# Adaln parameters of a transformer kernel: whole float32 matmuls in place of split parts

## The chip, the cores and the metric

The kernel runs on one core of a Trainium2 chip. Its time is the device time of one launch in microseconds (us). It has four compute engines with queues of their own, each of which works through its instructions in the order in which they stand: TensorE (PE, with its weight loads shown apart as PEld), VectorE (DVE), ScalarE (ACT) and GpSimd (POOL). SyncE (SP) issues most of the DMAs, also in order.

## The reference, cut to what matters

The reference is a transformer of two blocks on 256 tokens of 1024 features. The first block begins with the adaln parameters: a vector of conditions goes through silu and a matrix of 1024 x 6144, and the results shift, scale and gate the features.

```python
def adaln_params(cond, w_mod, b_mod):
    mod = jax.nn.silu(cond) @ w_mod + b_mod
    return mod.reshape(cond.shape[0], N_MOD, 1, cond.shape[-1])
...
mod = adaln_params(c, w_mod[layer], b_mod[layer])
mod_c = adaln_params(c_ctx[None, :], w_mod[layer], b_mod[layer])
h = modulate(x, norm1_g[layer], mod[:, 0], mod[:, 1])
hc = modulate(ctx, norm1_g[layer], mod_c[:, 0], mod_c[:, 1])
```

So the first 2048 parameters (shift and scale of the first norm) are wanted for two columns, c and c_ctx, and nothing of the first block's projections can start before shift and scale are there. Everything is float32.

## The kernel before

Activations lie transposed (features on the partitions, tokens on the free axis). Weights come from DRAM in tiles of 128 x 1024 (512 KB). A float32 product is carried by float32r passes: `split_w` (lines 107 to 116) makes of each raw weight tile a part hi by a cast on ACT (line 111) and a rest lo by a subtraction on DVE or POOL (line 115), and matmuls with hi and lo are summed in PSUM. A matmul of two operands that are plain float32 is one line in the program and two instructions in the trace.

The stretch around the change is the first 100 us. Three kinds of work share it:

- The adaln tiles. `mod_group` (line 299) runs for g = 0 to 3, four tiles `mraw` each; the text calls these sixteen tiles T0 to T15. Of each, hi and lo are made (on ACT and on DVE), and the two condition columns, as hi and lo parts in `sc4` of four columns, are the stationary operand while 512 weight columns move (line 308): 64 matmuls in all. The four rows of a group's result are copied out of PSUM (line 318, `mods`) and turned onto the partitions by small float32 matmuls with `fold` (line 323), and line 324 adds the bias into `mod`. The turn of groups 0 to 2 is issued in the next group.
- The filler. At places named in `PLACES`, one more tile of `mem_ahead` is issued, work that hangs on nothing near: keys of the memory attention, eight weight tiles with 24 matmuls each at line 137 (F0 to F7 here; F0's rest lo is made on DVE, of the others on POOL), then values, four tiles with 24 matmuls each at line 172 before the gates (V0 to V3). Two F tiles share the one PSUM bank `fill`, which line 1040 (`kvt`) empties on DVE.
- The norms of x and ctxT (squares on ACT at lines 214 and 217, sums on DVE at line 219, matmuls with ones at line 228) and the decay matrices of the retention (lines 388 to 416: a chain of small DVE steps `dlacc`, then, head by head, two DVE steps `decayt`, exponentials on ACT, and an addition on POOL).

When the last group is in `mod`, `scale_of` makes `modA`, `modulated` makes the normed input h in eight chunks (lines 246 to 248), and the gate blocks (line 137, `mm<-hh,whi`) begin the dense part of the kernel.

Within each engine the order is that of a scheduler which works over the whole program before it runs: it puts instructions of independent parts into one fixed row for each engine. At run time an instruction waits for its operands, and everything behind it on its engine waits with it. A tile's buffers also set the order: `raw` has three, the parts `whi` three and `wlo` two, `mraw` four.

Of the kernel before, what the change touches and what calls it, by code (L numbers as in the profile page):

```python
"""A two-part transformer in one launch.

Activations lie transposed, features on the partitions and tokens on the free axis, and stay in
SBUF from the first norm to the last. Weights stream through SBUF once. A float32 product is
carried by three float32r passes: each operand is split into a part that float32r holds exactly
and the rest (hi + lo), and hi*hi + hi*lo + lo*hi are accumulated in PSUM.
"""
# [8 lines left out]
F32 = mybir.dt.float32  # L16
F32R = mybir.dt.float32r
# [11 lines left out]
KC = 8  # L29
# [10 lines left out]
MRAW = 4  # L40
# [29 lines left out]
class Build:  # L70
# [15 lines left out]
    def banks(self, ctx, name):  # L86
        """The banks of one phase: mm and, by the phase, sc and aux or pairs of banks."""
        self.ps = ctx.enter_context(self.tc.tile_pool(name="psum" + name, bufs=2, space=PSUM))
# [5 lines left out]
    def after(self, ins, other):  # L94
        """Issue order only: no wait."""
        self.tc.add_manual_dep(ins.ins, other.ins.name,
                               mybir.DependencyInfo(mybir.DependencyClass.NoSync, mybir.DependencyReason.DATA),
                               reason="order")

# [18 lines left out]
    def weight(self, src, lo=None):  # L118
        """hi and lo of a weight tile. lo: the engine of the subtraction."""
# [7 lines left out]
    def mm3(self, out, pairs, first=True, last=True, late=False):  # L127
        """out += sum of w^T x over (w_hi, w_lo, x_hi, x_lo), three passes each; late: pair by pair."""
# [10 lines left out]
    def fill(self, n):  # L139
        """n tiles of the work that depends on nothing near."""  # L140
        for _ in range(n):
            next(self.filler, None)
# [6 lines left out]
    def block(self, out, src, x, cols=slice(None), lo=None, late=False, w=None):  # L149
        """out[128 n, tokens] = W block^T x, the weights stationary."""  # L150
# [8 lines left out]
    def natural_steps(self, tag, srcs, toks, done, lo=None):  # L159
        """x^T W with the tokens stationary, 256 columns of W (two tiles of srcs) at a time; two  # L160
        token blocks share a bank. done(n, i, bank) takes the columns n of the token blocks 2i, 2i + 1."""
# [26 lines left out]
    def rstd(self, pool, sums, n, tag, shape=(P, T), bufs=1, a=None, y=None, tables=False, behind=None):  # L188
        """(sums / n + eps) ** -0.5, a Newton step after the tables."""
# [19 lines left out]
    def track(self, x, m, tags=("acc", "accsq"), bufs=2):  # L209
        """Adds the squares of chunk m of eight to the sum over chunks; the last stays apart."""  # L210
# [10 lines left out]
    def tracked_norm(self, pool, tag, bank="aux", urgent=False, last=None, **kw):  # L221
        """rstd over the features of the chunks tracked, the same on every partition; last: behind the matmuls
        so far."""
# [17 lines left out]
    def modulated(self, pool, tags, x, r, A, Bv, h, cols):  # L241
        """h[:, :, cols] = x * r * A + B, split."""
# [8 lines left out]
    def gained(self, pool, x, gi, name="h"):  # L251
        """x * g (no rstd yet), split."""
# [37 lines left out]
    def mod_start(self, pool):  # L290
# [4 lines left out]
        self.sc4 = pool.tile([P, KC, 4], F32R, name="sc4")  # L295
        nc.vector.tensor_copy(self.sc4[:, :, 0:2], self.sc)
        nc.vector.tensor_sub(self.sc4[:, :, 2:4], self.sc, self.sc4[:, :, 0:2])

    def mod_group(self, pool, g):
        """512 of the adaln parameters, for c and for c_ctx: the rows of o are hi c, hi c_ctx, lo c, lo c_ctx."""  # L300
        nc, io = self.nc, self.io
        o = self.psum([P, 512])
        for q in range(4):
            wh, wl = self.split_w(self.raw(io["w_mod1"][g, q], pool, "mraw", MRAW), pool, "m", "v")
            for i, w in enumerate((wh, wl)):
                for kk in range(2):
                    k, m = 2 * q + kk, 4 - 2 * i
                    nc.tensor.matmul(o[:m], self.sc4[:, k, :m], w[:, kk * 512:kk * 512 + 512],
                                     start=k == 0 and i == 0, stop=k == 7, skip_group_check=True)
            if g == 0 and q == 0:  # L310
                self.load_constants()
                self.fold = pool.tile([4, 2], F32, name="fold")
                nc.vector.tensor_add(self.fold, self.ident[0:4, 0:2], self.ident[0:4, 2:4])
# [3 lines left out]
        s = pool.tile([4, 512], F32, name="mods", tag="mods", bufs=2)  # L317
        nc.vector.tensor_copy(s, o[:4])

        def turn():  # L320
            tr = self.psum([P, 4, 2])
            for j in range(4):
                nc.tensor.matmul(tr[:, j, :], s[:, j * P:(j + 1) * P], self.fold, start=True, stop=True)
            nc.vector.tensor_tensor(self.mod[:, 4 * g:4 * g + 4, :], tr,
                                    self.bmod[:, 4 * g:4 * g + 4, None].to_broadcast([P, 4, 2]), op=OP.add)

        if g == 3:
            turn()
        else:
            self.folding.append(turn)  # L330

    def mod_rest(self, pool, groups):
        """gate1, shift2, scale2, gate2 for c, a piece at a time."""
# [36 lines left out]
    def rope_out(self, pool, q, out, cos, sin):  # L370
        """out = q * cos + rot(q) * sin for q [128, 256] in SBUF; sin has the signs of rot, which swaps the halves
        of every 32 partitions."""
# [7 lines left out]
    def decay(self, pool, M):  # L380
        """M [j, t] for j in x and in ctx, by head: [128, 4 heads, 4 key chunks, 256]. The logarithms of the
        rates are not positive, so the smaller of the two exponents is the one for the sign of the distance."""
# [36 lines left out]
    def lam(self, pool, ls):  # L419
        """-lambda in the last column of ls."""  # L420
# [10 lines left out]
    def mixer(self):  # L431
        nc, io, tc = self.nc, self.io, self.tc
        with ExitStack() as ctx:
# [64 lines left out]
            def values(base):  # L498
                """[128 keys, 4 key blocks, 512], 256 columns at a time."""
# [10 lines left out]
            # differential attention  # L510
# [71 lines left out]
            # retention  # L582
# [54 lines left out]
    def residual(self, name, act, gate=None, nk=KC):  # L637
        """x += gate * (W^T act)."""
# [12 lines left out]
    def head_squared(self, pool, y):  # L651
        """y out of its bank, and its squares."""
# [7 lines left out]
    def head_norm(self, pool, y, g, out=None):  # L660
        """rms_norm over the partitions of y, times g; y as head_squared gives it."""
# [10 lines left out]
    def squared(self, pool, o, n):  # L672
        """o out of its bank, and its squares."""
# [8 lines left out]
    def qk_norm(self, pool, z, bd, g, out, n):  # L682
        """rms_norm over each 64 partitions of z as squared gives it: the first 256 columns in place, the others
        to out."""
# [11 lines left out]
    def peer(self):  # L696
        nc, io = self.nc, self.io
        with ExitStack() as ctx:
# [123 lines left out]
            def turn():  # L822
                """The selected keys by slot, and each gate as a float32r part and the ratio of its rest to that."""
# [30 lines left out]
            def hot(g):  # L854
                """The one-hot rows of the slots of TG tokens, with the gates in one of them, for two tokens at a time."""
# [92 lines left out]
            def collect(th):  # L948
                """x += gate * the transposed rows of acc, for the tokens of th."""
# [33 lines left out]
    def mem_kv(self, pool, mpool, l, key, value, norm=None):  # L983
        """k^T [128 d, 8, 256 m] and v [128 m, 2, 1024], two heads or 256 columns at a time; key and value
# [633 lines left out]
```

## Time and profile before

| what | value |
|---|---|
| median of 3 runs | 1934.56 us (1934.15 to 1935.23) |
| profiled execution, its span | 1934.6 us |
| PE busy over the span | 1838.1 us (95%) |
| DVE busy over the span | 1465.7 us (76%) |
| ACT busy over the span | 1043.2 us (54%) |
| POOL busy over the span | 587.3 us (30%) |
| first gate matmul | 95.51 us after the span's start |

Busy time is an engine's own; what sets the end is the chain of work, in which each step waits for one before it. In a row of the timeline the first two numbers are the start and the length in us, then come engine, line, operation, the tile written and those read, shapes, and how many such instructions in a row were merged (x8). A row that merges many shows the length from the first one's start to the last one's end. In a row of windows each engine has its busy us and, in brackets, how many instructions began; PEclk is the granted clock of TensorE, 1.00 for 2.4 GHz and 0.50 for 1.2 GHz.

### The profile page before, as it was taken

How to read it: one execution, taken by the hardware profiler on the slowest of the kernel's cores; microseconds unless marked ns; L12 is line 12 of the kernel's file. 1: busy time of each engine (PE TensorE's matmuls, PEld its weight loads, DVE VectorE, ACT ScalarE, POOL GpSimd, SP SyncE). 2: the span in 40 equal slices, each digit the busy share in tenths (PEclk: the TensorE clock that was granted, in tenths of full speed). 3: DMA queues.
4: the chain of work that ended last, by engine and by line, in shares of the span. 5: the costliest groups of instructions: out<-in, count | busy, mean ns of one | idle time of the engine just before them, and what ended most of it. 6: DMA issues, size and time to landing. Idle time of an engine off the chain costs nothing.

```text
span 1934.6 us, 34858 instructions
## 1 busy us (share of the span) xinstructions
PE 1838.1 (95%) x13232; PEld 1717.9 (89%) x13232; DVE 1465.7 (76%) x2646; ACT 1043.2 (54%) x1775; POOL 587.3 (30%) x508
## 2 busy tenths in 40 slices
PE   5899999994999999999999998999999999999997
PEld 4697788994999999878888878999999998999997
DVE  8988966999988999865555568676765578677664
ACT  5645534542777777554554455455554544555543
POOL 2511113782888999400000004222000213110001
PEclk8999999997999999999999998999999999999999
DMA  7672434452444444655555555553555553435553
GB/s 261 218 250 93 137 131 154 170 179 76 167 161 164 164 153 160 225 195 194 196 195 191 192 184 177 185 185 132 195 187 187 187 179 130 158 127 186 187 191 124
DMA packets 99768, 335.15 MB, mean 173 GB/s; under 512 B 12400, under 2 KB 13456, under 8 KB 99216
## 3 DMA queue, kind: packets, MB, share of 16 engines
q1 hardware_dynamic: 98160, 330.68, 49.5%
q8 instruction: 105, 1.72, 0.4%
q10 hardware_dynamic: 1440, 2.23, 0.3%
q14 instruction: 63, 0.52, 0.1%
HBM read 329.59 MB, written 3.28 MB: 172 GB/s over the span
## 4 chain that ended last, share of the span: by engine, by line
PE 69%; DVE 16%; POOL 9%; DMA 2%; issue 2%; ACT 2%; SPq 0%; DVEq 0%; ACTq 0%; POOLq 0%
PE mm L137 40%; PE pair L945 17%; POOL ohA L861 5%; PE mm L172 4%; POOL slots L882 3%; PE fill L137 2%; DVE wlo L115 2%; PE fill L172 2%; DVE slots L798 1%; DVE slots L795 1%; PE pair L876 1%; PE sc L137 1%; DVE slots L773 1%; PE aux L137 1%; DVE mlo L115 1%
## 5 line engine op out<-in xcount | busy, mean ns | idle before, releaser
L111 ACT CAST whi<-raw 128x1024 fp32r<-128x1024 f32 x564 | 591.4, 1050 | 517.5 <-PE mm L137 261.0
L115 DVE TENSOR_TENSOR wlo<-raw,whi 128x1024 fp32r<-128x1024 f32 x490 | 623.9, 1276 | 297.7 <-PE pair L945 129.3
L115 POOL TENSOR_TENSOR wlo<-raw,whi 128x1024 fp32r<-128x1024 f32 x74 | 186.5, 2522 | 199.1 <-PE mm L137 109.0
L861 POOL TENSOR_SCALAR ohA<-iota,selT 128x128 fp32r<-128x128 f32 x256 | 191.1, 762 | 53.2 <-ACT selT L829 32.5
L219 POOL TENSOR_TENSOR acc<-acc,accsq 128x256 f32<-128x256 f32 x42 | 37.9, 903 | 497.9 <-ACT accsq L217 497.9
L137 PE MATMUL mm<-hh,whi 128*128 128x256 f32 (+1 forms) x1184 | 180.0, 289 | 6.2 <-DVE ct L1243 4.4
L137 PE MATMUL mm<-hl,whi 128*128 128x256 f32 (+1 forms) x1184 | 177.1, 287 | 1.0 <-DVE hl L262 0.9
L137 PE MATMUL mm<-hh,wlo 128*128 128x256 f32 (+1 forms) x1184 | 175.7, 286 | 0.6 <-DVE wlo L115 0.6
L137 PE MATMUL mm<-h2h,whi 128*128 128x256 f32 x1152 | 167.6, 288 | 4.1 <-ACT h2h L247 4.0
L137 PEld LDWEIGHTS mm<-hh,whi 128*128 128x128 f32 x1184 | 156.5, 190 | 11.1 <-issue 6.8
L137 PE MATMUL mm<-h2h,wlo 128*128 128x256 f32 x1152 | 163.4, 284 | 0.0
L137 PE MATMUL mm<-h2l,whi 128*128 128x256 f32 x1152 | 162.4, 284 | 0.0
L945 PE MATMUL pair<-whi,acth 128*128 128x512 f32 x512 | 158.4, 391 | 1.0 <-ACT acth L937 1.0
L137 PEld LDWEIGHTS mm<-hh,wlo 128*128 128x128 f32 x1184 | 155.0, 190 | 4.4 <-issue 1.5
L945 PE MATMUL pair<-whi,actl 128*128 128x512 f32 x512 | 158.2, 390 | 0.3 <-DVE actl L938 0.3
L137 PEld LDWEIGHTS mm<-hl,whi 128*128 128x128 f32 x1184 | 155.2, 190 | 3.4 <-DVE hl L262 1.6
L945 PE MATMUL pair<-wlo,acth 128*128 128x512 f32 x512 | 157.8, 389 | 0.0
L137 PEld LDWEIGHTS mm<-h2h,whi 128*128 128x128 f32 x1152 | 151.9, 195 | 5.0 <-ACT h2h L247 4.8
L137 PEld LDWEIGHTS mm<-h2h,wlo 128*128 128x128 f32 x1152 | 150.1, 193 | 0.0
L137 PEld LDWEIGHTS mm<-h2l,whi 128*128 128x128 f32 x1152 | 149.3, 193 | 0.0
L1083 POOL TENSOR_TENSOR memk0l<-kvt,memk0h 128x512 fp32r<-128x512 f32 x4 | 6.4, 1611 | 378.9 <-ACT memk0h L1082 378.9
L945 PEld LDWEIGHTS pair<-whi,acth 128*128 128x128 f32 x512 | 95.5, 188 | 22.1 <-ACT acth L937 2.6
(416 smaller groups left out, 3454.2 us busy)
## 6 DMA issues: line engine op xcount, KB each, us to landing
raw<-peer_u SPq DMA_DIRECT2D x128, 512.0 KB, 3.5
raw<-peer_v SPq DMA_DIRECT2D x128, 512.0 KB, 3.4
raw<-ffn_gu SPq DMA_DIRECT2D x88, 512.0 KB, 3.6
raw<-ffn_dn SPq DMA_DIRECT2D x44, 512.0 KB, 3.5
raw<-w_mod SPq DMA_DIRECT2D x64, 256.0 KB, 4.1
raw<-conv_wi SPq DMA_DIRECT2D x24, 512.0 KB, 3.5
raw<-mem_wk SPq DMA_DIRECT2D x16, 512.0 KB, 4.5
mraw<-w_mod SPq DMA_DIRECT2D x16, 512.0 KB, 6.4
```

The costliest lines, as they stand in the source:

```text
L111: self.hi_copy = nc.scalar.copy(hi, raw)
L115: (nc.vector if plan == "v" else nc.gpsimd).tensor_sub(lo, raw, hi)
L137: self.matmul = nc.tensor.matmul(out, a, b, start=first and j == 0, stop=last and j == 3 * n - 1)
L172: self.matmul = nc.tensor.matmul(outs[i // 2][:, i % 2], a[:, k, :], b[:, w], start=k == 0 and s == 0 and i % 2 == 0, stop=k == 7 and s == ...
L219: self.adder.tensor_add(self.acc, self.acc, self.last)
L773: nc.vector.tensor_tensor(cand, vv[:, :, 0, :, None].to_broadcast([P, 2, 16, 16]), vv[:, :, 1, None, :].to_broadcast([P, 2, 16, 16]), op=O ...
L795: nc.vector.tensor_tensor(one, pb[:, :, :, None].to_broadcast([P, 2, 16, 16]), self.iota[:, None, None, 0:16].to_broadcast([P, 2, 16, 16]) ...
L798: nc.vector.tensor_tensor(one, one, ii[:, :, side, None, :].to_broadcast([P, 2, 16, 16]), op=OP.mult)
L861: nc.gpsimd.tensor_scalar(A[:, i], self.iota, selT[:, 1, t:t + 1], None, op0=OP.is_equal)
L876: nc.tensor.matmul(o[:, 2 * j + i], A[:, i], Bt[:, i], start=True, stop=True)
L882: getattr(nc, GMUL).tensor_mul(sl, lo[:, :, :done], sl)
L945: nc.tensor.matmul(acc[th][:, dh], x[:, tsl], wt[:, dh * 512:dh * 512 + 512], start=c == 0 and s == 0, stop=c == NCH - 1 and s == 2)
```

## The change

The tiles `mraw` are not split any more. The weights are the stationary operand (128 x 128 of a tile), and the two condition columns `sc` move, both plain float32; the result stands on the partitions at once, so the copy `mods`, the operand `fold` and the turn go, and line 315 adds the bias straight from the sum's bank. `MRAW` is 8 in place of 4. Docstrings and comments go too, which moves line numbers up by nine in the rest of the file.

```diff
-MRAW = 4
+MRAW = 8
...
-        self.sc4 = pool.tile([P, KC, 4], F32R, name="sc4")
-        nc.vector.tensor_copy(self.sc4[:, :, 0:2], self.sc)
-        nc.vector.tensor_sub(self.sc4[:, :, 2:4], self.sc, self.sc4[:, :, 0:2])
...
-        o = self.psum([P, 512])
+        o = self.psum([P, 4, 2])
         for q in range(4):
-            wh, wl = self.split_w(self.raw(io["w_mod1"][g, q], pool, "mraw", MRAW), pool, "m", "v")
-            for i, w in enumerate((wh, wl)):
-                for kk in range(2):
-                    k, m = 2 * q + kk, 4 - 2 * i
-                    nc.tensor.matmul(o[:m], self.sc4[:, k, :m], w[:, kk * 512:kk * 512 + 512],
-                                     start=k == 0 and i == 0, stop=k == 7, skip_group_check=True)
+            w = self.raw(io["w_mod1"][g, q], pool, "mraw", MRAW)
+            for kk in range(2):
+                k = 2 * q + kk
+                for j in range(4):
+                    c = kk * 512 + j * P
+                    nc.tensor.matmul(o[:, j, :], w[:, c:c + P], self.sc[:, k, :], start=k == 0 and j == 0,
+                                     stop=k == 7, skip_group_check=True)
             if g == 0 and q == 0:
                 self.load_constants()
-                self.fold = pool.tile([4, 2], F32, name="fold")
-                nc.vector.tensor_add(self.fold, self.ident[0:4, 0:2], self.ident[0:4, 2:4])
...
-        s = pool.tile([4, 512], F32, name="mods", tag="mods", bufs=2)
-        nc.vector.tensor_copy(s, o[:4])
-
-        def turn():
-            tr = self.psum([P, 4, 2])
-            for j in range(4):
-                nc.tensor.matmul(tr[:, j, :], s[:, j * P:(j + 1) * P], self.fold, start=True, stop=True)
-            nc.vector.tensor_tensor(self.mod[:, 4 * g:4 * g + 4, :], tr,
+
+        def place():
+            nc.vector.tensor_tensor(self.mod[:, 4 * g:4 * g + 4, :], o,
                                     self.bmod[:, 4 * g:4 * g + 4, None].to_broadcast([P, 4, 2]), op=OP.add)
 
         if g == 3:
-            turn()
+            place()
         else:
-            self.folding.append(turn)
+            self.folding.append(place)
```

The scheduler makes new rows of this. On DVE, around the first group's result and the first emptying of the filler's bank (`kvt`), there stood before:

```order
L394 TENSOR_TENSOR dlz_277<-dlz 128x8
L397 TENSOR_TENSOR dlacc<-dlacc,dlz_277 128x8
L398 TENSOR_SCALAR dlacc<-dlacc 128x8
L115 TENSOR_TENSOR mlo<-mraw,mhi 128x1024
L204 SCALAR_TENSOR_TENSOR mracc<-mracc,mry 128x256
...
L206 SCALAR_TENSOR_TENSOR mry<-mracc,mry 128x256
L397 TENSOR_TENSOR dlacc<-dlacc,dlz_277 128x8
L318 COPY mods<-mm 4x512
L1040 TENSOR_TENSOR kvt<-fill,mry 128x512
```

And now, at the same place:

```order
L385 TENSOR_TENSOR dlz_272<-dlz 128x8
L206 SCALAR_TENSOR_TENSOR mry<-mracc,mry 128x256
L388 TENSOR_TENSOR dlacc<-dlacc,dlz_272 128x8
L315 TENSOR_TENSOR mod<-mm,b_mod 128x8
L1031 TENSOR_TENSOR kvt<-fill,mry 128x512
L389 TENSOR_SCALAR dlacc<-dlacc 128x8
```

The addition into `mod`, which needs all of T0 to T3, stands where the copy `mods` stood, ahead of `kvt` and of nearly the whole chain `dlacc`; five of its steps stood ahead of `kvt` before and one does now.

On ACT, the cast `whi` of F3 and what stands ahead of it (the squares `acc` and `accsq`, the exponentials `decayM` and `decaye`) were before:

```order
L111 CAST mhi<-mraw 128x1024
L217 ACTIVATE accsq<-ctxT 128x256
L413 ACTIVATE decayM<-dist,dlfar,dllg 128x512
L111 CAST mhi<-mraw 128x1024
L415 ACTIVATE decaye<-dist,dlfar,dlneg 128x512
L111 CAST whi<-raw 128x1024
```

And now:

```order
L406 ACTIVATE decaye<-dist,dlfar,dlneg 128x512
L403 ACTIVATE decayM<-decayt 128x512
L214 ACTIVATE acc<-x 128x256
L217 ACTIVATE accsq<-x 128x256 x2
L214 ACTIVATE acc<-ctxT 128x256
L404 ACTIVATE decayM<-dist,dlfar,dllg 128x512
L217 ACTIVATE accsq<-x 128x256 x2
L111 CAST whi<-raw 128x1024
```

One head's `decaye` stood ahead of F3's cast before; now three heads' do (this is the third), with all the squares of x up to the fifth.

On PE, the last adaln tiles among the filler's matmuls stood before, from the second tile of group 2 on:

```order
L308 MATMUL mm<-mhi,sc_108 4x512 x2
L323 MATMUL mm<-fold,mods 128x2 x4
L308 MATMUL mm<-mlo,sc_108 2x512 x2
L308 MATMUL mm<-mhi,sc_108 4x512 x2
L137 MATMUL fill<-hmh,whi 128x256
L308 MATMUL mm<-mlo,sc_108 2x512 x2
L137 MATMUL fill<-hmh,whi 128x256 x7
L137 MATMUL fill<-hmh,wlo 128x256 x8
```

And now, from the last tile of group 1 to the last of group 3:

```order
L306 MATMUL mm<-sc,mraw 128x2 x32
L228 MATMUL aux<-acc,ones 128x256
L137 MATMUL fill<-hmh,whi 128x256 x8
L306 MATMUL mm<-sc,mraw 128x2
L137 MATMUL fill<-hmh,wlo 128x256 x8
L137 MATMUL fill<-hml,whi 128x256 x8
L306 MATMUL mm<-sc,mraw 128x2 x15
L137 MATMUL fill<-hmh,whi 128x256 x8
L306 MATMUL mm<-sc,mraw 128x2
L137 MATMUL fill<-hmh,wlo 128x256 x8
L137 MATMUL fill<-hml,whi 128x256 x8
L306 MATMUL mm<-sc,mraw 128x2 x23
```

Pairs of wide matmuls spread among the filler became runs of up to 32 narrow ones (four tiles), of which each is two instructions.

## Rows read from the trace of the kernel before

**Rows 1.** Windows of 10 us, with the view's heading row.
```profile
core 0: us, PE busy (x) PEld busy (x) DVE busy (x) ACT busy (x) POOL busy (x), PEclk, DMA share, GB/s
20.00:30.00 10.00, 9.20 (x42) 6.89 (x42) 9.67 (x23) 3.44 (x8) 2.40 (x1) 0.74 0.98 398
...
100.00:110.00 10.00, 10.00 (x85) 10.00 (x85) 10.00 (x19) 8.37 (x12) 0.00 (x0) 0.99 0.82 285
```

**Rows 2.** Chain of waits, 0 to 130 us: shares; then start, length, engine, line.
```profile
by line: PE mm L137 15.9%; DVE mlo L115 9.5%; PE mm L172 7.4%; DMA mraw<-w_mod 7.0%; issue 6.9%; PE fill L137 5.3%; DVE acc L219 4.7%; DVE modt L246 4.1%; DVE hl L248 3.8%; PE mm L308 3.0%; PE mm L323 2.4%; DVE decayt L411 2.3%; DVE mracc L
...
95.51 6.54 PE mm L137 x40
```

**Rows 3.** Instructions by line: count, then duration min/median/max in ns, first and last start.
```profile
L115 DVE TENSOR_TENSOR mlo<-mraw,mhi x16: 1203/1212/3324, 15.5 to 70.9; 128x1024 fp32r<-128x1024 f32 x16
...
L111 ACT CAST mhi<-mraw x16: 1027/1034/1050, 12.6 to 67.9; 128x1024 fp32r<-128x1024 f32 x16
...
L318 DVE COPY mods<-mm x4: 669/672/679, 29.2 to 77.2; 4x512 f32<-4x512 f32 x4
...
L323 PE MATMUL mm<-fold,mods x32: 246/246/267, 36.3 to 78.7; 4*128 4x2 f32 x32
```

**Rows 4.** Timeline of PE and PEld: runs of two-column matmuls, and weight loads.
```profile
57.50 1.05 PE L323 MATMUL mm<-fold,mods 4*128 4x2 f32 x8 [1.24 <-DVE mods L318]
...
131.81 0.95 PE L341 MATMUL mm<-ones,macc 128*128 128x2 f32 x8
...
8.19 0.29 PEld L137 LDWEIGHTS fill<-hmh,wlo 128*128 128x128 f32 x1 [0.15 <-DVE wlo L115]
...
11.53 0.19 PEld L137 LDWEIGHTS fill<-hmh,wlo 128*128 128x128 f32 x1
```

**Rows 5.** Timeline of PE: filler matmuls of F1 (two rows) and F3, then T6.
```profile
22.85 1.91 PE L137 MATMUL fill<-hmh,wlo 128*128 128x256 f32 x8
...
24.55 1.38 PE L137 MATMUL fill<-hml,whi 128*128 128x256 f32 x8
...
44.40 1.09 PE L137 MATMUL fill<-hml,whi 128*128 128x256 f32 x8
45.33 0.63 PE L308 MATMUL mm<-mhi,sc 128*4 128x512 f32 x2
```

**Rows 6.** Timeline of ACT, DVE and POOL: cast of F2, kvt, decay steps.
```profile
24.44 1.04 ACT L111 CAST whi<-raw 128x1024 fp32r<-128x1024 f32 x1
...
29.76 0.67 DVE L1040 TENSOR_TENSOR kvt<-fill,mry 128x512 f32<-128x512 f32 x1
...
31.15 0.42 DVE L219 TENSOR_TENSOR acc<-acc,accsq 128x256 f32<-128x256 f32 x1
31.49 0.16 DVE L397 TENSOR_TENSOR dlacc<-dlacc,dlz 128x8 f32<-128x8 f32 x1
...
37.37 0.81 ACT L415 ACTIVATE decaye<-dist,dlfar,dlneg 128x512 f32<-128x512 f32 x1
...
46.83 0.63 ACT L412 ACTIVATE decayM<-decayt 128x512 f32<-128x512 f32 x1 [4.13 <-DVE decayt L411]
...
38.26 2.29 POOL L416 TENSOR_TENSOR decayM<-decayM,decaye 128x512 f32<-128x512 f32 x1 [10.30 <-ACT decaye L415]
...
41.02 2.57 DVE L410 TENSOR_SCALAR decayt<-dist,dlneg 128x512 f32<-128x512 f32 x1
...
46.06 0.74 DVE L411 SCALAR_TENSOR_TENSOR decayt<-dist,dllg,decayt 128x512 f32<-128x512 f32 x1
```

**Rows 7.** Windows of 2 us around a run of L323.
```profile
56.00:58.00 2.00, 0.76 (x7) 0.50 (x5) 2.00 (x4) 2.00 (x3) 2.00 (x2) 1.00 0.86 244
...
60.00:62.00 2.00, 2.00 (x9) 1.80 (x8) 2.00 (x2) 0.71 (x1) 0.82 (x1) 0.50 0.95 369
```

**Rows 8.** Timeline of DVE and POOL after the last group.
```profile
78.98 0.17 DVE L324 TENSOR_TENSOR mod<-mm,b_mod 128x8 f32<-128x8 f32 x1 [1.14 <-PE mm L323]
...
81.94 2.70 POOL L115 TENSOR_TENSOR wlo<-raw,whi 128x1024 fp32r<-128x1024 f32 x1 [5.50 <-PE fill L172]
```

## The prediction, made before the change was run

> **What bounds the kernel now.** I read the windows first, then the chain of waits, then the engines' rows around the adaln tiles. From 100 us on PE is full (10.00 of 10 us) at a granted clock of 0.99 [rows 1], and the gate blocks that start this stretch begin at 95.51 [rows 2]. What matters here is therefore one number, the start of the gates: what comes behind it hangs on it, and I carry a shift of it to the end one for one. Ahead of it PE has gaps, and DVE is close to full (9.67 of 10 us from 20 to 30) [rows 1]. The chain from 0 to 130 us gives 9.5% to the subtractions `mlo`, 3.0% and 2.4% to the matmuls of lines 308 and 323 [rows 2]: what the change removes is on the path, with DVE ahead of PE. The last group is in `mod` at 78.98 + 0.17 = 79.2 us [rows 8], and the gates follow 16.4 us later.
>
> **What goes.** Sixteen `mlo` of 1.21 us, four `mods` of 0.67 us: 22.0 us of DVE. Sixteen casts of 1.03 us: 16.5 us of ACT. On PE 64 wide matmuls and 32 instructions of the turn [rows 3, 5]. With `mlo` gone what is late next is not the data but the order of what is left, below.
>
> **What comes.** 128 matmuls of 128 x 128 weights against two columns, two instructions each, since the turn's 16 of the program are 32 in the trace [rows 3]. Price of one: the run of eight at line 341, with 128 x 128 weights, is 0.95 us long, one of them 0.25 as at line 323, so (0.95 - 0.25) / 7 = 0.100 us from one to the next; at line 323 it is 0.115 [rows 4]. The run at 57.50 began at a clock of 1.00 [rows 7]. Such a run at the low clock is not in the trace: a weight load is 0.19 us after the clock rose and 0.29 before [rows 4], and eight filler matmuls take 24.55 - 22.85 = 1.70 us from start to start at the low clock, 0.213 each, and 45.33 - 44.40 = 0.93 at the high one, 0.116 each [rows 5]. So 0.100 is the low bound, twice that, 0.20, the high one, and a tile of 16 costs 1.6 to 3.3 us; all sixteen 25.6 to 52 us. I let the clock decide between them (step 3). The 64 wide ones, two in 0.63 us [rows 5], were 20 us at most, with the turn's 32 x 0.115 = 3.7 on top: PE's work does not shrink, and at the low clock it more than doubles.
>
> The Trainium skill, "TensorE: Matmul & The Clock Gate", section "LDWEIGHTS (loading the stationary operand)", gives a load's time as its columns over 1.2, which is 107 ns for 128 at either clock. Here loads of one size took 0.19 and 0.29 us, so the trace does not agree that the clock leaves them alone. By that rule, an estimate, the narrow matmuls of step 3 would cost 17 us whatever the clock, and the sum would come out near +11 instead of +16.
>
> **Step 1: the first group.** T0 starts behind F0 at 12.7 as before. F1 starts about 0.9 us earlier, since one `mlo` ahead of the memory norm on DVE is gone; it ended at 24.55 + 1.38 = 25.9 [rows 5], now 25.0. T2 and T3 follow, 3.2 us: T3 ends at 28.2 (31.6 at the low clock). Only then can DVE add the first group into `mod`, and `kvt` stands right behind it: 0.17 + 0.67 and a little, 29.1; before it started at 29.76 [rows 6]. No gain so far. But ACT's cast for F2 now stands behind `kvt`'s DMA, so it runs near 29.2, where before it ran at 24.44 [rows 6], and POOL's rest comes 2.7 us [rows 8] behind it.
>
> **Step 2: F3 behind the decay chain.** The row of ACT puts F3's cast behind three heads of exponentials and five squares of x, and these wait for DVE. From `kvt` at 29.1: 17 steps `dlacc` at about 0.20 and three more, 4.1 us, to 33.2. Then head by head, since `decayt` and `decaye` have two buffers between them: two exponentials 1.6; an addition on POOL 2.29; an exponential 0.81; an addition 2.29; an exponential 0.81 and 0.63; the fourth head's two `decayt`, 2.57 beside POOL and 0.74; two sums of 0.42 with the squares behind them, 1.3; the cast 1.03 [rows 6]: 14.1, less 0.7 for overlaps of neighbours on ACT, 13.4. F3's cast ends at 46.6, POOL's rest at 49.2, and its last 16 matmuls take 1.9 to 3.4 us: F3 ends at 51.5. It ended at 44.40 + 1.09 = 45.5 [rows 5]. What hid all this before was that F3's cast stood behind one head only. PE meanwhile has just F2, T4 and T5, and idles for some 5 us.
>
> **Step 3: F3's end to T15's end.** PE then has, in this order: T6, the norm of x, F4, F5, T7 to T10, the norm of ctxT, F6, T11, T12, F7, T13 to T15. At the high clock: 96 filler matmuls at 0.117, 11.2 us; 160 narrow ones at 0.100, 16.0. Apart from these 1.8 us for the two norms and 3.1 for a wait: F6's cast stands behind the ctxT norm's logarithm on ACT, so PE waits for a DVE step, that logarithm, the cast (1.03) and, after eight matmuls, POOL's 2.70. Sum 32 at the high clock; at the low one 2 x 27.2 + 4.9 = 59. Which of these? Before the clock fell to 0.50 (60 to 62 us), PE was busy in 56 to 58 for only 0.76 us [rows 7], and from 57.50 on that was the run of line 323 [rows 4]; in 20 to 30 us, with the filler beside waits, it was 0.74 on average [rows 1]. The new runs are longer (up to 64 instructions) than any of these. I take 0.72, next to that row: 27.2 / 0.72 = 37.8, plus 4.9, 43 us. T15 ends at 51.5 + 43 = 94.5; before, the same stretch ended at 79.0.
>
> **Step 4: from T15 to the gates.** V0's cast now stands behind the first chunks of h on ACT, so all four V tiles come after T15: POOL's first rest starts 3.0 us after `mod` (as the one at 81.94 did, after 78.98), four at 2.70 make 10.8, and V3's 24 matmuls 2.8 [rows 8]: 16.6. The modulation on DVE runs beside it, with fewer norm steps in between. It was 16.4, so nothing is won: gates at 94.7 + 16.6 = 111.3 against 95.5.
>
> **Sum.** +15.8 us. The span is 1934.6 and the median 1934.56, so no correction: 1950.4. Eight `mraw` buffers cost nothing and bring nothing, since SP's later tiles stand behind `raw` tiles which wait for POOL's rests of F2 to F4 (steps 1 and 2); T7 to T15 are there by the time PE comes to them.
>
> **Rivals.**
> - *The clock stays high.* Back-to-back narrow matmuls may keep it. Then step 3 is 32, F3 ends at 51.1, T15 at 83.2, gates at 100.0: +4.5, 1939. For it: a run of line 323 itself began at 1.00. Against it: what the clock did after that run [rows 7]. The Trainium skill, same page, section "What's actually happening", says the gate follows how busy PE has been of late; if a stream of loads counts as busy, this is that case, and no run here shows so long a stream.
> - *The clock stays low throughout.* Step 3 is 59, T3 3.4 later and F3 at 56.0, so T15 ends at 115.0 and the gates start at 131.8: +36, 1971. Against it: F4 with F5, and F6, are dense filler, and dense filler raised it before.
> - *DVE's time is all that counts* (the faster side). If steps 1 and 2 do not bite, because ACT and POOL come to F2's and F3's tiles in time, the chain's 9.5% of 130 us goes: 12.4 us, and PE's work (25.6 against 23.7 at most) hides in its gaps: 1922. It decides if F3 ends before about 40 us. For it: DVE is near full before 80 us. Against it: rows 6, the fixed order.
> - *Part of it is made up later*: PE's backlog after the gates finds DVE further ahead, the shift shrinks to under 4 us: 1936. Against it: PE is full from 100 us on [rows 1].
>
> **Chances.** The forecast (mixed clock, +7 to +26) 0.57; high clock 0.12, which lies on the edge and which I count 0.08 slower, 0.04 the same; low clock 0.08; faster rival 0.16; made up later 0.07, of it 0.06 the same. About 0.2%, 3.9 us, is what can be told from no change. Slower 0.57 + 0.08 + 0.08 + 0.01 = 0.74, same 0.10, faster 0.16. The range 1928 to 1967 leaves out most of the faster rival and of the low clock; the forecast's own range is 1942 to 1961.
>
> **What would show it.** Right: the first `mod` row near 28 us with `kvt` right behind; F3's cast on ACT near 46; PE idle ahead of F3; runs of line 306 stepping at 0.10 in one clock and about 0.2 in the other, and the granted clock falling during T7 to T10; T15's end past 85; gates near 111. Wrong: F3 ending before 42, or T15 before 79, or the narrow matmuls stepping otherwise than 0.10 to 0.21; and a gap before the gates much shorter than 16 us.

## The result, and the profile after

The changed kernel takes 1959.87 us (median of 4 runs, 1958.97 to 1961.74) against 1934.36 for the kernel before beside it: 1.0133 times, 95% interval 1.0119 to 1.0147, or +25.5 us. The forecast was slower, 1950, with a range up to 1967: the direction and the range hold, the size was 15.8 and is 25.5. The profiled execution has a span of 1958.0 us against 1934.6. Its time was 1959.78 us: in every run on record the time is 1.7 to 2.3 us above the span of the same execution. By this, an estimate, the execution profiled before took some 1936.4 us, which is 2 us above its kernel's median, so "no correction" in the prediction's sum was wrong by that much, and +23.4 in the spans goes with +25.5 in the medians.

First the windows of 10 us of the changed kernel, columns as in [rows 1]:

```profile
40.00:50.00 10.00, 4.50 (x22) 4.21 (x23) 8.18 (x9) 6.67 (x14) 6.12 (x3) 0.54 0.44 162
...
60.00:70.00 10.00, 9.34 (x54) 8.61 (x53) 0.77 (x3) 0.17 (x1) 0.00 (x0) 0.64 0.53 183
...
80.00:90.00 10.00, 10.00 (x63) 10.00 (x62) 0.69 (x1) 0.00 (x0) 0.00 (x0) 0.66 0.11 44
...
100.00:110.00 10.00, 6.49 (x41) 6.28 (x39) 9.82 (x12) 3.94 (x7) 6.42 (x3) 0.81 0.57 194
```

DVE, which was near full before [rows 1], has 0.77 and 0.69 us of work in two of these windows (9.45 and 10.00 in the kernel before): the change did free it, and nothing used it. PE either waits (busy for 4.50 of 10 us from 40 to 50) or is full, or nearly so, at a clock of about 0.65. The timeline of PE, in which the last column is the idle time ahead and what ended it:

```profile
12.58 1.84 PE L306 MATMUL mm<-sc,mraw 128*128 128x2 f32 x16
...
15.04 3.58 PE L306 MATMUL mm<-sc,mraw 128*128 128x2 f32 x16 [0.62 <-DMA mraw<-w_mod]
...
45.07 2.07 PE L137 MATMUL fill<-hmh,whi 128*128 128x256 f32 x8 [5.76 <-ACT whi L111]
...
49.34 1.10 PE L137 MATMUL fill<-hml,whi 128*128 128x256 f32 x8
...
58.54 9.73 PE L306 MATMUL mm<-sc,mraw 128*128 128x2 f32 x64
...
71.23 2.08 PE L137 MATMUL fill<-hmh,whi 128*128 128x256 f32 x8 [1.90 <-ACT whi L111]
...
95.78 0.58 PE L172 MATMUL fill<-whi,hmh 128*128 128x256 f32 x1 [2.86 <-ACT whi L111]
...
98.37 0.58 PE L172 MATMUL fill<-wlo,hmh 128*128 128x256 f32 x1 [1.80 <-POOL wlo L115]
...
103.01 0.41 PE L172 MATMUL fill<-wlo,hmh 128*128 128x256 f32 x1
...
111.16 0.58 PE L172 MATMUL fill<-whi,hmh 128*128 128x256 f32 x1 [4.67 <-ACT kvt L1035]
...
118.23 1.12 PE L137 MATMUL mm<-hh,whi 128*128 128x256 f32 x8
...
133.14 2.00 PE L137 MATMUL mm<-hh,whi 128*128 128x512 f32 x8
```

These are T0 at the high clock (1.00) and T1 at the low one (0.51), F3's wait, F3's end (it was 44.40 + 1.09 in [rows 5], now 50.4), T7 to T10 in one run, F6, V0's two waits, V0's last matmul, V2's wait, and the gates, which begin at 118.23. The 95.51 of [rows 2], which the table of the kernel before calls its first gate matmul, is its ninth, from which on PE is busy without a gap; the first is at 92.04. As a mark that all kernels here share I use the last row, the first gate block of 512 columns. In the kernel before the two are:

```profile
92.04 0.87 PE L137 MATMUL mm<-hh,whi 128*128 128x256 f32 x6
...
110.47 2.00 PE L137 MATMUL mm<-hh,whi 128*128 128x512 f32 x8
```

The block moved by 22.7 us and the span by 23.4, so what stands behind the gates hangs on them nearly one for one, as the prediction took it. The rows on DVE, ACT and POOL that answer to [rows 6, 8]:

```profile
27.30 0.17 DVE L315 TENSOR_TENSOR mod<-mm,b_mod 128x8 f32<-128x8 f32 x1 [4.37 <-PE mm L306]
27.39 0.68 DVE L1031 TENSOR_TENSOR kvt<-fill,mry 128x512 f32<-128x512 f32 x1
...
29.60 2.38 DVE L389 TENSOR_SCALAR dlacc<-dlacc 128x8 f32<-128x8 f32 x1
...
92.96 0.17 DVE L315 TENSOR_TENSOR mod<-mm,b_mod 128x8 f32<-128x8 f32 x1 [5.81 <-PE mm L306]
...
104.08 2.62 DVE L246 SCALAR_TENSOR_TENSOR modt<-x,modA,nry 128x256 f32<-128x256 f32 x1
...
107.28 2.56 DVE L246 SCALAR_TENSOR_TENSOR modt<-ctxT,modA,nry 128x256 f32<-128x256 f32 x1
```

```profile
34.33 0.81 ACT L404 ACTIVATE decayM<-dist,dlfar,dllg 128x512 f32<-128x512 f32 x1 [4.82 <-DVE dlfar L395]
...
43.99 1.03 ACT L111 CAST whi<-raw 128x1024 fp32r<-128x1024 f32 x1
...
109.87 0.51 ACT L247 ACTIVATE hh<-modt,bx 128x256 fp32r<-128x256 f32 x1 [2.63 <-DVE modt L246]
110.29 0.82 ACT L1035 ACTIVATE kvt<-fill,rn 128x256 f32<-128x256 f32 x2
```

```profile
29.59 2.37 POOL L115 TENSOR_TENSOR wlo<-raw,whi 128x1024 fp32r<-128x1024 f32 x1 [11.82 <-ACT whi L111]
...
35.93 1.27 POOL L407 TENSOR_TENSOR decayM<-decayM,decaye 128x512 f32<-128x512 f32 x1 [3.98 <-ACT decaye L406]
...
95.86 4.98 POOL L115 TENSOR_TENSOR wlo<-raw,whi 128x1024 fp32r<-128x1024 f32 x2 [19.66 <-ACT whi L111]
103.66 2.75 POOL L115 TENSOR_TENSOR wlo<-raw,whi 128x1024 fp32r<-128x1024 f32 x1 [2.83 <-ACT hh L247]
106.72 2.84 POOL L115 TENSOR_TENSOR wlo<-raw,whi 128x1024 fp32r<-128x1024 f32 x1 [0.30 <-PE fill L172]
```

The last addition into `mod` is at 93.0 (79.0 before). From there to the gates it is 25.3 us, where the forecast had 16.6. V2 waits 4.67 us because `kvt`, which empties the filler's one bank, stands on ACT behind the chunks `hh`, and these wait for `modt` on DVE, which takes 2.6 us in place of 0.45 in the two rows above, where it begins while one of POOL's rests runs. A last view: windows cut at the steps' ends, from F3's end to T15's, then from T15 to the gates.

```profile
50.40:93.00 42.60, 40.23 (x261) 39.08 (x259) 15.46 (x23) 8.05 (x16) 8.72 (x4) 0.73 0.40 143
...
93.00:118.20 25.20, 15.95 (x96) 15.45 (x97) 22.27 (x32) 11.59 (x19) 10.57 (x4) 0.72 0.45 148
```

### The profile page after: what moved, and what is told of

Same layout as the page of the kernel before. It is cut to its first block, busy times and chain, and to the rows that moved or that the text cites. A ratio compares the mean times of both kernels' runs of the same rounds, so it can differ in the third digit from the quotient of the medians.

```text
span 1958.0 us, 35118 instructions
## 1 busy us (share of the span) xinstructions
PE 1860.0 (95%) x13392; PEld 1751.4 (89%) x13392; DVE 1447.1 (74%) x2623; ACT 1029.1 (53%) x1759; POOL 582.2 (30%) x508
## 4 chain that ended last, share of the span: by engine, by line
PE 70%; DVE 15%; POOL 9%; ACT 2%; DMA 2%; issue 1%; SPq 0%; DVEq 0%; POOLq 0%; ACTq 0%
PE mm L137 39%; PE pair L936 17%; POOL ohA L852 5%; PE mm L172 3%; POOL slots L873 3%; PE fill L172 2%; PE fill L137 2%; DVE wlo L115 1%; DVE slots L789 1%; PE mm L306 1%; DVE slots L786 1%; PE pair L867 1%; PE sc L137 1%; DMA raw<-w_mod 1%; DVE slots L764 1%
## 5 line engine op out<-in xcount | busy, mean ns | idle before, releaser
L936 PEld LDWEIGHTS pair<-whi,actl 128*128 128x128 f32 x512 | 95.4, 188 | 22.4 <-DVE actl L929 3.0
```

The source lines that it names most:

```text
L936: nc.tensor.matmul(acc[th][:, dh], x[:, tsl], wt[:, dh * 512:dh * 512 + 512], start=c == 0 and s == 0, stop=c == NCH - 1 and s == 2)
```

## The experiments

Theory A: the loss has two sources, the clock, which falls in the runs of two-column matmuls, and the order of the rows on ACT and DVE. B: PE simply has more instructions. C: the clock alone. All ratios are to the kernel before on the same chip, and gains against the changed kernel are differences of ratios times 1934 us. T15 is the last group's `mod`, or T15's end on PE where DVE came to `mod` later; block is the start of the 512-column block. T15, block and span are those of one profiled execution: its time is 4 us above the run's median in w_wide, 4 below it in v_values_first, 7 below it in dmwv_order_wide, and within 2 us of it in the others.

| run | median us | ratio (95%) | T15 | block | span |
|---|---|---|---|---|---|
| before | 1934.4 | 1 | 79.0 | 110.5 | 1934.6 |
| changed | 1959.9 | 1.0133 (1.0119 to 1.0147) | 93.0 | 133.1 | 1958.0 |
| w_wide | 1941.8 | 1.0040 (1.0025 to 1.0056) | 76.1 | 120.4 | 1944.2 |
| d_casts_first | 1947.3 | 1.0070 (1.0057 to 1.0084) | 84.4 | 123.8 | 1945.6 |
| m_kvt_first | 1953.9 | 1.0108 (1.0090 to 1.0126) | 90.6 | 132.1 | 1951.9 |
| v_values_first | 1951.1 | 1.0093 (1.0078 to 1.0108) | 90.3 | 125.1 | 1945.4 |
| v_rest_on_dve | 1948.8 | 1.0087 (1.0072 to 1.0102) | 94.9 | 128.5 | 1946.2 |
| dmv_order | 1942.5 | 1.0047 (1.0029 to 1.0065) | 82.0 | 118.7 | 1939.9 |
| dmwv_order_wide | 1938.8 | 1.0025 (1.0015 to 1.0035) | 66.9 | 113.5 | 1930.1 |
| dmv_rest_on_dve | 1938.3 | 1.0026 (1.0015 to 1.0036) | 82.1 | 115.3 | 1935.7 |
| best_order_wide | 1921.8 | 0.9937 (0.9924 to 0.9949) | 67.6 | 96.8 | 1921.1 |
| four_buffers | 1958.8 | 1.0135 (1.0115 to 1.0155) | 95.2 | 136.7 | 1955.9 |
| best_order_narrow | 1939.6 | 1.0022 (1.0007 to 1.0037) | 85.1 | 116.3 | 1938.5 |
| before_order | 1934.3 | 1.0005 (0.9995 to 1.0014) | 74.6 | 109.8 | 1930.5 |

Span less block lies between 1816.6 and 1824.9 in all fourteen profiled executions: apart from these 8 us the start of the gates decides the time. A few us at the block of a single profile can therefore not be read as time: four_buffers has the changed kernel's time with its block 3.6 us later.

**w_wide: the clock.** The same weights, loads and number of instructions, with 128 columns moving.

```diff
+        self.scw = pool.tile([P, KC, 64, 2], F32, name="scw")
+        nc.vector.tensor_copy(self.scw, self.sc[:, :, None, :].to_broadcast([P, KC, 64, 2]))
...
-                    nc.tensor.matmul(o[:, j, :], w[:, c:c + P], self.sc[:, k, :], ...
+                    nc.tensor.matmul(o[:, j, :], w[:, c:c + P], self.scw[:, k], ...
```

> The moving operand of the adaln matmuls is 128 columns wide in place of 2 (the two condition columns, repeated 64 times by one more copy on DVE early on); weights, loads, number and order of the instructions stay. Theory A (the change lost time through the clock, which falls during the runs of two-column matmuls, and through the fixed order of ACT and DVE): the granted clock stays at 1.00 from T7 to T15, the steps of line 306 stay at 0.107 us and none at 0.214 are left from 50 us on; the stretch from F3's end to T15's end shrinks from 42.6 to about 33 us, V0 and V1 run at the high clock, and the time falls by 8 to 13 us, to 1947 to 1952. Theory B (PE simply has more instructions to carry out, and the low clock is an accident beside it): the columns are an added cost, each of the 256 instructions grows by 0.05 us or more, +10 us or more, or no change within 3 us. Theory C (the clock is all there is): the whole +25.5 us of the change goes, 1935 to 1938.

Measured: 18 us less than the changed kernel, more than expected. Its window from F3's end to T15's, T0 and the run of T7 to T10, and the first gate matmul:

```profile
46.70:76.10 29.40, 29.34 (x259) 29.18 (x258) 9.87 (x17) 9.85 (x16) 13.27 (x6) 1.00 0.68 237
```

```profile
12.83 1.95 PE L308 MATMUL mm<-scw,mraw 128*128 128x128 f32 x16
...
54.27 7.31 PE L308 MATMUL mm<-scw,mraw 128*128 128x128 f32 x64
...
96.98 0.98 PE L137 MATMUL mm<-hh,whi 128*128 128x256 f32 x2 [7.43 <-ACT hh L247]
```

259 instructions in 29.4 us at a clock of 1.00, where the changed kernel has 261 in 42.6 at 0.73 (two matmuls of the norms and F6's wait of 1.90 us among them); 64 of them 7.31 against 9.73 us. More columns cost next to nothing (T0: 1.95 us in place of 1.84, both at the high clock) and the number of instructions was no cost in itself: B falls. But T15 ends 2.9 us earlier than in the kernel before and the time is still 0.4% longer, so the clock up to T15 is not all, as C has it. The scheduler made other rows for the wide form: V0 and V1 stand ahead of the norms on PE, and PE waits 7.43 us for `hh`. A scheduler that sees other lengths gives another order, so this run moves two things. That C falls is shown by the next runs, which keep two columns.

**d_casts_first, m_kvt_first, v_values_first: the order, one coupling each.** `after` adds an order without a wait; `casts` lists the casts in order of issue.

```diff
 # d: the same for the other exponentials and the squares
+            self.after(nc.scalar.activation(e2, d, AF.Exp, ...), self.casts[4])
 # m
+            if g == 0:
+                self.after(add, self.kvt)
 # v
+            if tags == ("modt",) and cols.start == 0:
+                self.after(hh, self.casts[9 if k < 2 else 10])
```

> On ACT the casts of F3 and F4 are put ahead of the exponentials of the decay matrices and of the squares of x and ctxT, as nothing of these is wanted early; the rest of the order follows. Theory A: F3's end moves from 50.4 to 42 to 45 us, since its cast no longer waits for the decay chain; part of it comes back later, since the norms of x and ctxT and the matmuls on PE behind them start later; gates 3 to 7 us earlier, time 1953 to 1957. Theory B (PE's added instructions are the cost): no change within 3 us, since PE has the same work. Theory C (clock alone): no change within 3 us.

> On DVE the addition of the first group into mod is put behind the first kvt, which empties the filler's bank, where the changed kernel had it ahead (so kvt need not wait for T2 and T3 on PE). Theory A: kvt starts up to 2 us before its 27.39 us, F2's cast (28.47) and F2 as much earlier; the wait ahead of F3, which hangs on the decay chain on DVE and ACT, swallows most of it: 0 to 3 us gained in all, 1957 to 1960. Theories B and C: no change within 2 us.

> On ACT the casts of V0 and V1 are put ahead of the first chunks of h, and that of V2 ahead of the third. Theory A: the waits ahead of V0 (2.86 and 1.80 us) and part of the one ahead of V2 (4.67 us) go, the time from mod's last group to the first gate matmul falls from 25.2 to 16 to 20 us, and the time by 5 to 9 us, 1951 to 1955; the emptying of the filler's bank on ACT still stands behind six chunks of h, so that part of V2's wait may stay. Theories B and C: no change within 3 us, since PE's work and the clock ahead of mod stay as they are.

d: 12 us less, more than expected, and hardly by the clock: from F3's end to T15's it is 0.74 on average, against 0.73 in the changed kernel, and PE has no wait there. On ACT the casts of F3 and F4 now follow F2's at once, and F3's last filler matmuls on PE end at 45.2 (50.4):

```profile
30.04 1.04 ACT L112 CAST whi<-raw 128x1024 fp32r<-128x1024 f32 x1 [8.57 <-DVE dlacc L394]
...
30.99 1.99 ACT L112 CAST whi<-raw 128x1024 fp32r<-128x1024 f32 x2
```

```profile
44.08 1.09 PE L139 MATMUL fill<-hml,whi 128*128 128x256 f32 x8
```

v: 8 us less, with the block 34.8 us behind the last `mod` in place of 40.2; 2.6 us of the rest are T15, which came earlier. m: 5 us less where 0 to 3 were expected. `kvt` did start earlier (24.10 against 27.39), but the block moved by 1.0 us only. Its ratio is lower than the changed kernel's, but the intervals overlap and its profile shows no gain of that size at the gates, so what this coupling cost stays open.

**v_rest_on_dve: POOL beside DVE.** One argument changed.

```diff
-                                      lambda n, i, o: value(n, o, rn), FILL_LO)
+                                      lambda n, i, o: value(n, o, rn), "v" if l == 0 else FILL_LO)
```

> The rests wlo of the value tiles V0 to V3 (and of the four value tiles issued later) are made on DVE in place of POOL; the order ahead of the last adaln group stays word for word. Theory A (step 4 grew because DVE's modt and hl take 2.3 to 2.6 us instead of 0.4 to 0.5 where POOL works beside them, and because V0 waits for POOL's rest): no rest on POOL between mod and the gates, modt and hl all near 0.45 us, the first gate matmul 17 to 20 us behind mod's last group in place of 25.2, time 5 to 9 us lower, 1951 to 1955. Rival D (DVE itself is the bound between mod and the gates): eight or so rests of 1.21 us are added to it there, the gates come later and the time rises by 2 to 8 us. Theory C (the clock is all there is): within 3 us.

Measured: 9 us less, though T15 ended 1.9 us later in this execution. On DVE a pair of `modt` takes 0.88 us throughout, and the gates begin 19.3 us behind `mod`:

```profile
106.31 0.88 DVE L246 SCALAR_TENSOR_TENSOR modt<-x,modA,nry 128x256 f32<-128x256 f32 x2
...
111.65 1.22 DVE L115 TENSOR_TENSOR wlo<-raw,whi 128x1024 fp32r<-128x1024 f32 x1
```

```profile
114.21 1.11 PE L137 MATMUL mm<-hh,whi 128*128 128x256 f32 x8
```

The order ahead of `mod` is the same here, and the clock from `mod` to the gates hardly moves (0.74 against 0.72), so the 6.6 us that the block comes nearer to `mod` (33.6 us in place of 40.2) are step 4's: more work on the engine that waits was the cheaper way (rival D falls). The span is 11.8 us shorter and the block only 4.6 us earlier, so 7 us of it lie behind the block; the edit also moves four later rests, and what they bring was not tried by itself.

**Combinations.** Three edits of order; the same with wide columns; the same with the value tiles' rests on DVE.

> The three edits of order together (casts of F3 and F4 ahead of the decay exponentials and squares; kvt ahead of the first addition into mod; casts of V0 to V2 ahead of the chunks of h); the narrow matmuls as in the changed kernel. One by one they saved 12, 5 and 8 us. Theory A: they act in different places, of which the first two follow one another in the same wait (F3's), so 15 to 22 us go, time 1938 to 1945; what is left, 5 to 11 us, is the clock in the runs of narrow matmuls. Theory C (clock alone): the single gains were luck of where the low clock fell, together no more than the largest: 1946 to 1950.

> The same three edits of order and the moving operand 128 columns wide. Theory A: clock and order are all that the change lost, and what it took off DVE and ACT then shows: 1924 to 1933, at or below the kernel before. Rival E (the rows that the scheduler makes for wide matmuls spoil the stretch between mod and the gates, as in the run with wide columns alone, where the gates came 29 us behind T15's end): 1934 to 1942.

> The three edits of order, narrow matmuls, and the rests of the value tiles on DVE. Theory A: 2 to 5 us less than the three edits alone, 1934 to 1941, since the casts of V0 to V2 are early already and only POOL's 2.7 us for each rest and DVE's slow steps beside it go. Rival D: 2 to 8 us more than the three edits alone.

The three edits save 17 us together (25 one by one): they overlap, as expected. The rests on DVE save about 4 more (the intervals, 1.0029 to 1.0065 and 1.0015 to 1.0036, overlap, so this gain is not shown by the times alone). With wide columns rival E came true: T15 ends at 66.9 and not 82.0, but the block begins at 113.5, so that 5 of these 15 us are left. The steps `macc` of the second block's parameters stood ahead of `mod` and the norms on DVE and waited there for their weights, so that `mod` came 9.5 us behind T15:

```profile
72.88 3.62 DVE L356 SCALAR_TENSOR_TENSOR macc<-raw,sc,macc 128x512 f32<-128x512 f32 x2 [2.81 <-DMA raw<-w_mod]
...
76.42 0.16 DVE L325 TENSOR_TENSOR mod<-mm,b_mod 128x8 f32<-128x8 f32 x1
```

**best_order_wide: both sources mended.** To wide columns, the three edits and the rests on DVE come two lines:

```diff
-                self.at("h")
                 r1 = self.norm(p1, self.x, "nr", bufs=2)
                 r2 = self.norm(p1, ctxT, "nr", bufs=2)
+                self.at("h")
...
-                    nc.vector.tensor_scalar(acc, w, s, None, op0=OP.mult)
+                    self.after(nc.vector.tensor_scalar(acc, w, s, None, op0=OP.mult), self.hl)
```

> The three edits of order, wide columns and the value tiles' rests on DVE, and two more edits of order for the stretch between T15 and the gates: the value tiles are issued behind the norms of x and ctxT (so that the norms' matmuls stand ahead of V0 on PE and not behind V1), and the first steps macc on DVE (the adaln parameters of the second block) are held behind the last chunk hl of x. In the run with order and wide columns T15 ended at 66.9 us, but its 512-column gate block began only at 113.5. Theory A (the shift of the gates is what counts, and clock and order set it): that block begins 32 to 37 us behind T15's end, as in the kernel before, at 99 to 106 us, against 110.5 in the kernel before, and the time is 4 to 11 us below it, 1923 to 1930. Rival E (the macc steps and weight loads that were moved are wanted soon after, and what is won at the gates is lost behind them): within 4 us of the kernel before, 1930 to 1938.

Measured: 1921.78 us (1918.70 to 1923.33), 0.9937 of the kernel before, below both kernels and 1 us below the range expected; the block comes 29.1 us behind `mod`, sooner than the 32 to 37 expected. The last group's `mod` on DVE, then T7 to T10 and the block on PE:

```profile
67.65 0.17 DVE L325 TENSOR_TENSOR mod<-mm,b_mod 128x8 f32<-128x8 f32 x1 [3.50 <-PE mm L316]
```

```profile
45.77 7.31 PE L316 MATMUL mm<-scw,mraw 128*128 128x128 f32 x64
...
96.79 2.63 PE L139 MATMUL mm<-hh,whi 128*128 128x512 f32 x14
```

**best_order_narrow and before_order: the two controls.** The run above with two columns moving; and the kernel before with the edits of order that apply to it (not m, which concerns an addition that the kernel before makes elsewhere).

> As the run with all edits of order and wide columns (1921.8 us), but with two columns moving. The scheduler gives somewhat different rows for it. Theory A: the clock falls again in the runs of T7 to T10 and T13 to T15, T15 ends 8 to 14 us later than in that run, and the time is 8 to 14 us higher, 1930 to 1936, near the kernel before. Rival G (with the order mended the clock costs nothing, since the norms and casts are what the gates wait for): within 4 us, 1919 to 1926.

> The kernel before, with split adaln tiles and four buffers, and the same edits of order: casts of F3 and F4 ahead of the decay exponentials and squares, casts of V0 to V2 ahead of the chunks of h, value tiles behind the norms with their rests on DVE, macc held behind the chunks of x. Theory A (the order was fitting in the kernel before, so that mending it there brings little, and what the change takes off DVE and ACT is worth something once it is ordered well): within 5 us of the kernel before, 1928 to 1938, slower than the mended changed kernel. Rival H (the gain of the mended kernel is the order's alone): 1919 to 1925.

With two columns the time is 0.85% or 16 us above the wide run, and T15 is 17.4 us later; more than the 8 to 14 expected. T7 to T10 of the narrow run:

```profile
51.39 10.83 PE L314 MATMUL mm<-sc,mraw 128*128 128x2 f32 x64
```

And the stretch from F1's first matmul to T15's last in each run, the narrow one first:

```profile
19.54:85.04 65.50, 65.50 (x403) 65.17 (x401) 29.68 (x69) 23.52 (x43) 19.97 (x10) 0.68 0.61 209
```

```profile
19.72:67.60 47.88, 47.75 (x407) 47.45 (x406) 33.77 (x66) 23.18 (x40) 20.64 (x10) 0.97 0.85 299
```

PE is busy throughout in both, with 403 and 407 instructions begun, and its timeline shows no wait. So although the scheduler's rows differ here too, it is not their order that parts the two stretches but the granted clock, 0.68 against 0.97 (rival G falls); the busy share hides it. The kernel before gains nothing from the edits of order: 1.0005, T15 at 74.6 and the block 0.7 us earlier. So the 12 us of the mended kernel are not the order's alone; the change itself is worth them once it is ordered for and kept at the high clock (rival H falls). The edits were chosen for the changed kernel; that no other order would help the kernel before is not shown.

**four_buffers.** `MRAW = 4`.

> Four mraw buffers in place of eight, all else as in the changed kernel. Prediction's view (eight buffers cost and bring nothing, since SP's later tiles stand behind raw tiles that wait for POOL's rests): within 2 us of the changed kernel, 1957 to 1962. Rival (the tiles' early loads take DMA time from F's and V's weights): 2 to 5 us faster. Rival (late loads starve PE in the long runs of narrow matmuls): 2 to 6 us slower.

1.0135 against 1.0133: eight buffers neither cost nor bring anything that can be measured, though the interval, 1.0115 to 1.0155, leaves 4 us either way.

## Why the prediction was right, and where its size was off

*Steps 1 to 3 held in their sums, in part by luck.* First group: `mod` at 27.30, and `kvt` right behind it ends at 28.07 (forecast 28.2 and 29.1). F3's cast ended at 45.0 and F3 at 50.4 (forecast 46.6 and 51.5); PE waited 5.76 us ahead of it (forecast some 5). Inside step 2 two terms were off in opposite directions. From `kvt`'s end to the first exponential (34.33) it took 6.3 us in place of 4.1, with one `dlacc` of 2.38 us beside POOL's rest. From there to the cast's end it took 10.7 us in place of 13.4, since POOL's additions took 1.27 us and not 2.29, and no `decayt` took the 2.57 that was charged. That their sum came within 1.6 us is luck.

F3's end to T15's end: 42.6 us at a mean clock of 0.73 (forecast 43 at 0.72); F6's wait is there too. The clock's alternation is what the forecast said; the 0.72 itself was taken from a window with other work in it, so that it fits so well is in part luck as well. The prices of a narrow matmul were 0.106 at the high clock (T0, (1.84 - 0.25) / 15, one by itself being 0.25) and 0.214 at the low one (T1, (3.58 - 0.37) / 15, the longest by itself being 0.37), inside the 0.10 to 0.20 taken from [rows 4, 5] but for the upper end. (The granted clock reads 1.00 around both loads of [rows 4]; that the one at 8.19 was at the low clock shows in the matmuls behind it, 0.213 from one to the next against 0.118 at 11.64.) T15's end came out at 93.0 (forecast 94.5): +14.0 of the +23.4 by then. That F3's wait was a cause, and not a companion, is what d shows, and for the clock it is the pair best_order_wide and best_order_narrow.

The Trainium skill, "TensorE: Matmul & The Clock Gate", section "LDWEIGHTS (loading the stationary operand)", gives a load's time as its columns over 1.2, 107 ns for 128, and names no clock. T0's step of 0.106 agrees with that, T1's 0.214 at the low clock does not. By that rule, an estimate, the 160 narrow instructions of step 3 would have cost 17 us; their rows in the trace add up to some 22. That the prediction's +11 by this rule lies so far under +25.5 is for the most part step 4's doing and not the rule's.

*Step 4 was mis-sized.* The forecast: "POOL's first rest starts 3.0 us after `mod`", "four at 2.70 make 10.8, and V3's 24 matmuls 2.8", 16.6 in all. Measured, from `mod` at 92.96: the first rest starts 2.9 us later; the four take 13.7 us, not 10.8, because the third waits 2.83 us. Its row puts this wait down to `hh`, but a rest also needs one of the two `wlo` buffers: V0's last matmul, which reads the first of them, ends at 103.01 + 0.41, 0.24 us ahead of the third rest, as V1's last ends 0.23 us ahead of the fourth, and in d_casts_first and v_values_first the profile names PE for the same wait (2.82 and 2.67 us). V0's matmuls were at the low clock then (0.50 from 98.0 to 103.7). Behind the four rests come 1.6 us more until `kvt` has emptied the bank; then not 24 but 48 matmuls, V2's and V3's, 7.1 us with a part at the low clock in place of 2.8. In sum 25.3: 8.7 us more than forecast. With T15 1.5 us early, the gates came 6.9 us behind the forecast 111.3, which is nearly all of the 7.6 us that the span's +23.4 lies above +15.8. The 16.4 us to which the forecast compared its 16.6 ran to the ninth gate matmul; to the first it was 12.9. By the block, `mod` lay 31.5 us ahead in the kernel before and 40.2 in the changed one, again 8.7 us more.

I counted POOL's rests as the train that sets the end, and left out what holds that train up and who empties the bank: `kvt` of the values is on ACT, behind the chunks `hh`, and these behind DVE steps that POOL's rests stretch. The slow step was in front of me (2.57 for a `decayt` beside POOL, in [rows 6]); I charged it to step 2 and not to step 4. v_values_first and v_rest_on_dve each take a part of it away: the block comes 5.4 and 6.6 us nearer to `mod`. Their gains of 8 and 9 us are not step 4's alone (T15 2.6 us earlier in the one, 7 us behind the block in the other).

The stretched steps end just behind POOL's: `modt` from 104.08 ends at 106.70 and POOL's rest at 106.41, `modt` from 107.28 at 109.84 and the rest at 109.56. The Trainium skill, "SBUF — State Buffer", section "Terms", says that DVE and GpSimd share a pair of ports which one holds for its full instruction while the other blocks; the trace agrees, and v_rest_on_dve, with no rest on POOL there, has none of these long steps.

*The rivals.* High clock throughout (1939) and low clock throughout (1971) were both wrong, as the clock alternated. "DVE's time is all that counts" (1922) failed at the point that was named for it, F3's end before 40. With both sources mended the kernel does reach 1921.8; that the size fits is not shown to be for that rival's reason. "Made up later" failed: span less block hardly moves.

Open: what m gains behind the gates, why span less block differs by up to 8 us between runs, and how much of w's own gain is the other order of its rows.

## What to carry to other kernels

Where engines work through fixed rows, taking work off the fullest one is worth only what the instructions behind it can use: look for who empties the bank and which cast stands behind whom, and mend the order with the change. For a long run of matmuls with very few moving columns read the granted clock, not the busy share; here repeating two columns to 128 cost one copy and took 16 us off. A run that widens an operand can also change a scheduler's rows: compare with a control that has the same edits of order on both sides.

## What the runs showed of the hardware

- 128 moving columns cost a float32 matmul with 128 x 128 weights hardly more time than 2 do at the high clock: T0's 16 instructions took 1.95 us with 128 columns (w_wide), 0.112 from one to the next, and 1.84 us with 2 (the changed kernel), 0.106.
- A DVE step of 128 x 8, 0.17 us otherwise, took 2.38 us when it began with a rest on POOL (29.60 beside 29.59 + 2.37 above): the length of the small step does not protect it.
- In the rows above a rest of 128 x 1024 takes 1.22 us on DVE and 2.37 to 2.84 on POOL.
